# Eight weight buffers at eight different offsets modulo 512 bytes

## The chip, the core and the metric

The kernel runs on one core of a Trainium2 chip. The core has a matrix engine (TensorE, PE in the profile; its weight loads are PEld), a vector engine (VectorE, DVE), a scalar engine (ScalarE, ACT), GpSimd (POOL) and SyncE (SP), whose queue issues most of the DMAs here. They share SBUF, an on-chip memory of 128 partitions, in which a tile has the same byte range in every partition; TensorE writes its products to PSUM. The metric is the time of one execution on the device in microseconds (us).

## What is computed

A decoder trunk of two layers for 256 tokens and a model width of 2048, all in float32. Each layer is a mixer and then a gated feed-forward network (5632 wide) with a short convolution on its gate. The first mixer is a dilated attention of 8 heads beside a convolution module; the second is attention with forget gates (16 heads).

```python
for l in range(DEPTH):
    h = rmsnorm(x, norm_mix[l])
    if l % 2 == 0:
        x = x + even_mixer(h, positions, ev_w_in[e], ev_conv_w[e], ...)
    else:
        x = x + odd_mixer(h, od_w_in[o], od_b_f[o], od_w_out[o])
    h = rmsnorm(x, norm_ffn[l])
    x = x + conv_ffn(h, ffn_w_up[l], ffn_conv_w[l], ffn_w_down[l])
return rmsnorm(x, norm_final)

def conv_ffn(h, w_up, conv_w, w_down):
    g, u = jnp.split(h @ w_up, [D_FF], axis=-1)
    g = causal_dwconv(g, conv_w)
    return (jax.nn.silu(g) * u) @ w_down
```

Nearly all the work is in the products of `h` and of what is made of it with weight matrices, some 410 MB that are read once from HBM.

## The kernel before

A float32 product is made from rounded parts. Every weight and every activation is split into a high part, rounded to the type fp32r that TensorE is given, and a low part, the rest; a product is high x high + high x low + low x high.

**The weights' stream.** `stream` (L78) is a generator that every product draws its weights from. For four k-tiles (128 rows each) of a panel of 512 columns it issues one DMA of 1 MB from SyncE into a tile `raw` (three buffers, L85). Each half of it, two k-tiles or 1024 columns of a partition, is split: ScalarE's cast makes the high part `whi` (L93) and VectorE subtracts it from `raw` to make the low part `wlo` (L94). Of `whi` and `wlo` there are four buffers each, in turn, in the pool `wp`. A buffer has 1024 float32 values, 4096 bytes in each partition, and they lie one behind another, so all eight begin at the same offset modulo 512 bytes: 64. The three `raw` buffers begin at 64 as well.

**Who reads the parts.** `panel_b` (L108) has the weights as the stationary operand, 128 x 128 at a time, and the activations as the moving one. In its wide form (L102, issued in a written order by `in_order`) each block of weights gives a pair: the high part with a 512-wide moving operand, which holds the activations' high and low parts side by side, and the low part with the 256 columns of the high part alone. In its narrow form (L122 to L124) it issues three matmuls of 256 columns. `panel_a` and the last product (`mm_a`, L136 to L138) have it the other way round: the activations are stationary, and 512 columns of weights move. The blocks of a buffer are 512 bytes apart, so every block keeps its buffer's offset modulo 512.

**The activations' tiles.** `xs`, the split input of a mixer or a network, begins at 64 modulo 512. It feeds the products ag, q, k, v and fl of the mixers and g and u of the networks (the letters stand behind `acc_`, `whi_`, `wlo_` and `raw_` in the profile). The attention's output `y` feeds the output projections: at 288 oa and ob in the first layer, at 416 oc in the second. The network's hidden tiles `hp` feed the down projection: at 448 in the first layer (d, `panel_b`), at 0 in the second (d by `panel_a`, then e).

**The last product.** The second layer's second group of the down projection (e, in `down1`) draws the last four k-tiles of its four panels into rooms taken from other tiles and, by `from_weights`, from `whi` and `wlo`.

The order on TensorE is that of the products; ScalarE and VectorE split weights ahead of it, as far as the four buffers allow, and do the normalisations, the softmax and the convolutions between.

Of the kernel before, what the change touches and what calls it, by code (L numbers as in the profile page):

```python
# [10 lines left out]
F32R = mybir.dt.float32r  # L11
# [5 lines left out]
P = 128  # L17
# [12 lines left out]
KC = 2  # L30
# [11 lines left out]
def trunk(ctx, tc, a):  # L42
# [4 lines left out]
    wp = ctx.enter_context(tc.tile_pool(name="wp", bufs=4))  # L47
# [4 lines left out]
    def misc(name):  # L52
        return pms.tile([P, 512], F32, tag="misc", name=name)
# [16 lines left out]
    def fill_in(after):  # L70
        pace[1] += pace[0]
        with tc.issue_after(after.ins), tc.high_priority(offset=-BEHIND):
            while waiting and pace[1] >= 1:
                waiting.pop(0)()
                pace[1] -= 1
        pace[1] = min(pace[1], 1.0)

    def stream(src_of, nk, width, name, dk=4, room=None):  # L78

        half = KC * 512 // width  # L80
        for c in range(0, nk, dk * 512 // width):
            n = dk * 512 // width
            raw = wp.tile([P, 2 * KC * 512], F32, tag="raw", name=f"raw_{name}_{c}", bufs=3)
            rv = raw[:, :n * width].rearrange("p (k c) -> p k c", k=n)
            loads.append(nc.sync.dma_start(out=rv, in_=src_of(c, n)))  # L85
            for h in range(0, n, half):
                if room is None:
                    hi = wp.tile([P, half, width], F32R, tag="whi", name=f"whi_{name}_{c + h}")
                    lo = wp.tile([P, half, width], F32R, tag="wlo", name=f"wlo_{name}_{c + h}")
                else:  # L90
                    hi, lo = room(f"{name}_{c + h}")
                with tc.high_priority(offset=AHEAD):
                    S.copy(hi, rv[:, h:h + half, :])  # L93
                    last = V.tensor_tensor(out=lo, in0=rv[:, h:h + half, :], in1=hi.bitcast(F32), op=ALU.subtract)  # L94
                fill_in(last)
                yield list(range(c + h, c + h + half)), hi, lo
# [38 lines left out]
    def mm_a(o, hi, lo, xh, xl, first, last):  # L135
        PE.matmul(o, xh, hi, start=first, stop=False)  # L136
        PE.matmul(o, xh, lo, start=False, stop=False)  # L137
        PE.matmul(o, xl, hi, start=False, stop=last)  # L138

    def panel_a(src_of, x2, kts, name):  # L140

        acc = [pacc.tile([P, 512], F32, tag="acc", name=f"acc_{name}_{t}") for t in range(2)]
        for ks, hi, lo in stream(src_of, len(kts), 512, name):
            for t in range(2):
                ts = slice(t * P, (t + 1) * P)
                for j, k in enumerate(ks):
                    x = x2(kts[k])
                    mm_a(acc[t], hi[:, j, :], lo[:, j, :], x[:, 0, ts], x[:, 1, ts], k == 0, k == len(kts) - 1)
        return acc

    def cols(w, panel, k0=0):

        def part(c, n):
            kt = k0 // P + c
            return w[panel, kt // 4, :, kt % 4:kt % 4 + n, :]
        return part
# [125 lines left out]
    with ExitStack() as ph:  # L282
# [72 lines left out]
        with tc.high_priority(offset=400):  # L355
            for i in range(4):
                t, h = divmod(i, 2)
# [259 lines left out]
    def x_back():  # L617
        for kt in range(0, KT, 2):
            tx = misc(f"tb_{kt}")
            for t in range(2):  # L620
                for k in range(2):
                    PE.transpose(tx[:, t * T + k * P:t * T + (k + 1) * P], xT[:, kt + k, t * P:(t + 1) * P], ident)
            S.copy(o[:, :, kt * P:(kt + 2) * P], tx.rearrange("p (t c) -> p t c", t=2))
        S.dma_start(out=gb, in_=a["norm_final"].partition_broadcast(P))

    def add_o(acc, t, i):
        cs = slice(512 * i, 512 * (i + 1))
        V.tensor_tensor(out=o[:, t, cs], in0=acc, in1=o[:, t, cs], op=ALU.add)

    def down1(gi, w_dn, k0, kts, g2, fp):  # L630
        if gi == 0:
            x_back()
            for i in range(4):
                acc = panel_a(cols(w_dn, i, k0=k0), g2, kts, f"d1{gi}{i}")
                for t in range(2):
                    add_o(acc[t], t, i)
            return


        with tc.issue_after(copies[-1].ins):  # L640
            S.activation(dummy, ones[:, 0:1], AF.Sqrt)
        acc = [[None, None] for i in range(4)]
        for b, (i, t) in enumerate((i, t) for i in range(4) for t in range(2)):
            acc[i][t] = misc(f"acc_e{i}{t}") if b < 3 else pacc.tile([P, 512], F32, tag="acc", name=f"acc_e{i}{t}")
        n = len(kts)

        def rows(i, t, at, ks, hi, lo):
            for j, k in enumerate(ks):
                kt, ts = kts[at + k], slice(t * P, (t + 1) * P)
                mm_a(acc[i][t], hi[:, j, :], lo[:, j, :], g2(kt)[:, 0, ts], g2(kt)[:, 1, ts], at + k == 0, at + k == n - 1)  # L650

        def part(i, at, k, **kw):
            return stream(cols(w_dn, i, k0=k0 + at * P), k, 512, f"e{i}_{at}", dk=k, **kw)

        for at in range(0, n - 4, 4):
            for i in range(4):
                for got in part(i, at, 4):
                    for t in range(2):
                        rows(i, t, at, *got)


        def from_gate(nm):
            return [fp.tile([P, KC, 512], F32R, tag=tag, name=f"{w}_{nm}", bufs=2) for tag, w in (("gp", "whi"), ("cv", "wlo"))]

        def from_hidden(nm):
            both = fp.tile([P, 4, 2, T], F32R, tag="hp", name=f"wboth_{nm}", bufs=6).rearrange("p a b t -> p (a b t)")
            return [both[:, 1024 * h:1024 * (h + 1)].rearrange("p (k c) -> p k c", k=KC) for h in range(2)]

        def from_weights(nm):
            return [wp.tile([P, KC, 512], F32R, tag=w, name=f"{w}_{nm}") for w in ("whi", "wlo")]  # L670

        def from_raw(nm):
            both = wp.tile([P, 2 * KC * 512], F32, tag="raw", name=f"wboth_{nm}", bufs=3).bitcast(F32R)
            return [both[:, 1024 * h:1024 * (h + 1)].rearrange("p (k c) -> p k c", k=KC) for h in range(2)]

        rooms = [from_gate] * 2 + [from_hidden] + [from_weights] * 4 + [from_raw]
        at = n - 4
        last = [list(part(i, at, 4, room=lambda nm: rooms.pop(0)(nm))) for i in range(4)]
        for t in range(2):
            for i in range(4):  # L680
                for got in last[i]:
                    rows(i, t, at, *got)
                add_o(acc[i][t], t, i)
                cs = slice(512 * i, 512 * (i + 1))
                S.activation(junk[:, 512 * (i % 2):512 * (i % 2) + 512], o[:, t, cs], AF.Square, accum_out=fs[:, t, i:i + 1])
                if i < 3:
                    V.tensor_tensor(out=o[:, t, cs], in0=o[:, t, cs], in1=gb[:, cs], op=ALU.mult)
            V.reduce_sum(out=sf[:, t:t + 1], in_=fs[:, t, :], axis=AX.X)
            rf = rsqrt_cols(sf[:, t:t + 1], 1.0 / D, f"fin{t}", 1)
            for i in (1, 0, 3, 2):  # L690
                cs = slice(512 * i, 512 * (i + 1))
                if i == 3:
                    V.scalar_tensor_tensor(out=o[:, t, cs], in0=o[:, t, cs], scalar=rf, in1=gb[:, cs], op0=ALU.mult, op1=ALU.mult)
                elif i == 1:
                    V.tensor_scalar(out=o[:, t, cs], in0=o[:, t, cs], scalar1=rf, scalar2=None, op0=ALU.mult)
                else:
                    S.activation(o[:, t, cs], o[:, t, cs], AF.Copy, scale=rf)
                nc.sync.dma_start(out=a["out"][t * P:(t + 1) * P, cs], in_=o[:, t, cs])
# [63 lines left out]
```

## Time and profile before

| | |
|---|---|
| time, median of 3 runs | 2226.87 us (2223.21 to 2228.09) |
| profiled execution | 2227.58 us, of it span 2225.8 us |
| granted TensorE clock, mean | 0.997 |
| mean DMA rate | 186 GB/s |
| HBM read | 409.84 MB |

The span is the time from the first instruction of the program to the last one's end. A group of the profile is the set of instructions of one line, engine, operation and tiles; behind its count stand busy time, mean ns of one, and the idle time of the engine just ahead of them with what ended it. The end of a matmul in the profile is modelled, and successive matmuls overlap, so the pace of TensorE is read from starts: the length of a stretch divided by the matmuls that began in it. A stretch is written as start:end in us from the span's beginning. The count behind TensorE's busy time is of all matmuls that touch the stretch, so one that began before it can be among them.

### The profile page before, as it was taken

The page shows a single profiled execution, that of the slowest core. Times are in us where ns is not written, and L with a number is a line of the kernel's source. Part 1 is how long each engine was busy: PE and PEld are TensorE (multiplying, and loading weights), DVE is VectorE, ACT ScalarE, POOL GpSimd, SP SyncE. Part 2 cuts the span into 40 slices and gives each one's busy share as a digit, 9 for nine tenths or more (in the row PEclk, how much of TensorE's full clock was granted, in tenths as well). Part 3 has the DMA queues.
Part 4 walks back from the last instruction along what each step waited for, and adds up shares of the span by engine and source line. Part 5 has one row for each costly group of instructions (what it writes and reads, how often), then busy time and mean ns, then how long its engine had stood idle before and what let it go on. Part 6 is the DMA issues. An engine that isn't in the chain of part 4 may idle for free.

```text
span 2225.8 us, 31945 instructions
## 1 busy us (share of the span) xinstructions
PE 2206.7 (99%) x12778; PEld 1944.7 (87%) x12778; DVE 1490.9 (67%) x2284; ACT 1118.0 (50%) x1579; POOL 15.6 (1%) x50
## 2 busy tenths in 40 slices
PE   8999999999999999999999999999999999999998
PEld 8999988888888888888888888888888888888886
DVE  6999987766755576666665555666776644677745
ACT  6567665544443445444554454455454433444534
POOL 0000000000000000000000000000000000000000
PEclk9999999999999999999999999999999999999999
DMA  8554445555555555555545444455555555555553
GB/s 284 184 186 173 152 174 186 189 190 190 189 188 189 189 189 190 189 190 189 191 156 187 171 171 169 178 184 200 184 189 191 192 194 192 189 190 189 190 189 133
DMA packets 60230, 414.08 MB, mean 186 GB/s; under 512 B 7232, under 2 KB 7936, under 8 KB 11184
## 3 DMA queue, kind: packets, MB, share of 16 engines
q1 hardware_dynamic: 59328, 410.72, 51.8%
q8 instruction: 100, 1.64, 0.3%
q10 hardware_dynamic: 144, 1.05, 0.1%
q0 software_dynamic: 608, 0.26, 0.1%
q14 instruction: 50, 0.41, 0.1%
HBM read 409.84 MB, written 2.10 MB: 185 GB/s over the span
## 4 chain that ended last, share of the span: by engine, by line
PE 98%; DMA 1%; ACT 1%; DVE 0%; SPq 0%; issue 0%; ACTq 0%; DVEq 0%
PE acc_g L102 22%; PE acc_u L102 22%; PE acc_d L102 11%; PE acc_oc L102 4%; PE acc_q L102 4%; PE acc_k L102 4%; PE acc_ob L102 2%; PE acc_d L136 2%; PE acc_d L138 2%; PE acc_v L137 2%; PE acc_v L138 2%; PE acc_v L136 2%; PE acc_d L137 2%; PE acc_e L137 2%; PE acc_e L136 2%; PE acc_e L138 2%
## 5 line engine op out<-in xcount | busy, mean ns | idle before, releaser
L102 PE MATMUL acc_g<-xs,whi_g 128*128 128x512 f32 x1408 | 490.7, 392 | 0.0
L102 PE MATMUL acc_u<-xs,whi_u 128*128 128x512 f32 x1408 | 489.8, 392 | 0.0
L102 PE MATMUL acc_g<-xs,wlo_g 128*128 128x256 f32 x1408 | 394.1, 280 | 0.0
L102 PE MATMUL acc_u<-xs,wlo_u 128*128 128x256 f32 x1408 | 393.4, 279 | 0.0
L94 DVE TENSOR_TENSOR wlo_g<-raw_g,whi_g 128x1024 fp32r<-128x1024 f32 x176 | 215.3, 1223 | 165.5 <-ACT whi_g L93 165.2
L102 PEld LDWEIGHTS acc_g<-xs,whi_g 128*128 128x128 f32 x1408 | 263.6, 187 | 59.5 <-issue 0.5
L102 PEld LDWEIGHTS acc_u<-xs,whi_u 128*128 128x128 f32 x1408 | 263.5, 187 | 58.8
L93 ACT CAST whi_u<-raw_u 128x1024 fp32r<-128x1024 f32 x176 | 185.7, 1055 | 254.5 <-PE acc_u L102 142.1
L94 DVE TENSOR_TENSOR wlo_u<-raw_u,whi_u 128x1024 fp32r<-128x1024 f32 x176 | 215.4, 1224 | 124.4 <-ACT whi_u L93 124.4
L93 ACT CAST whi_g<-raw_g 128x1024 fp32r<-128x1024 f32 x176 | 185.3, 1053 | 213.8 <-PE acc_g L102 99.1
L94 DVE TENSOR_TENSOR wlo_d<-raw_d,whi_d 128x1024 fp32r<-128x1024 f32 x136 | 166.5, 1224 | 162.4 <-ACT whi_d L93 162.0
L102 PEld LDWEIGHTS acc_g<-xs,wlo_g 128*128 128x128 f32 x1408 | 265.8, 189 | 0.1
L102 PEld LDWEIGHTS acc_u<-xs,wlo_u 128*128 128x128 f32 x1408 | 265.7, 189 | 0.0
L93 ACT CAST whi_d<-raw_d 128x1024 fp32r<-128x1024 f32 x136 | 143.0, 1051 | 212.3 <-PE acc_d L102 126.7
L102 PE MATMUL acc_d<-hp,whi_d 128*128 128x512 f32 x704 | 247.9, 394 | 0.0
L102 PE MATMUL acc_d<-hp,wlo_d 128*128 128x256 f32 x704 | 199.1, 283 | 0.0
L102 PEld LDWEIGHTS acc_d<-hp,whi_d 128*128 128x128 f32 x704 | 132.2, 188 | 31.4 <-issue 1.1
L102 PEld LDWEIGHTS acc_d<-hp,wlo_d 128*128 128x128 f32 x704 | 132.4, 188 | 0.0
L102 PE MATMUL acc_q<-xs,whi_q 128*128 128x512 f32 x256 | 90.5, 395 | 0.0
L102 PE MATMUL acc_oc<-y,whi_oc 128*128 128x512 f32 x256 | 90.3, 395 | 0.0
L102 PE MATMUL acc_k<-xs,whi_k 128*128 128x512 f32 x256 | 88.9, 391 | 0.0
L94 DVE TENSOR_TENSOR wlo_v<-raw_v,whi_v 128x1024 fp32r<-128x1024 f32 x48 | 58.7, 1222 | 45.1 <-ACT whi_v L93 44.4
(317 smaller groups left out, 4200.1 us busy)
## 6 DMA issues: line engine op xcount, KB each, us to landing
raw_g<-in_ffn_w_up SPq DMA_DIRECT2D x88, 1024.0 KB, 4.7
raw_u<-in_ffn_w_up SPq DMA_DIRECT2D x88, 1024.0 KB, 4.8
raw_d<-in_ffn_w_down SPq DMA_DIRECT2D x68, 1024.0 KB, 4.7
raw_e<-in_ffn_w_down SPq DMA_DIRECT2D x20, 1024.0 KB, 4.8
raw_q<-in_od_w_in SPq DMA_DIRECT2D x16, 1024.0 KB, 4.8
raw_k<-in_od_w_in SPq DMA_DIRECT2D x16, 1024.0 KB, 4.8
raw_v<-in_od_w_in SPq DMA_DIRECT2D x16, 1024.0 KB, 4.8
raw_oc<-in_od_w_out SPq DMA_DIRECT2D x16, 1024.0 KB, 4.8
```

The lines of the kernel that those rows point to most:

```text
L93: S.copy(hi, rv[:, h:h + half, :])
L94: last = V.tensor_tensor(out=lo, in0=rv[:, h:h + half, :], in1=hi.bitcast(F32), op=ALU.subtract)
L102: i = PE.matmul(*args, **kw).ins
L136: PE.matmul(o, xh, hi, start=first, stop=False)
L137: PE.matmul(o, xh, lo, start=False, stop=False)
L138: PE.matmul(o, xl, hi, start=False, stop=last)
```

## The change

The tiles `whi` and `wlo` get 16 more float32 values each (64 bytes in each partition), which nothing reads or writes. A new function `split_pair` makes both tiles and gives views of their first 1024 values; `stream` and `from_weights` call it.

```diff
+    def split_pair(nm, half, width):
+
+        both = [wp.tile([P, KC * 512 + 16], F32R, tag=w, name=f"{w}_{nm}") for w in ("whi", "wlo")]
+        return [t[:, :KC * 512].rearrange("p (k c) -> p k c", k=half) for t in both]
+
     def stream(src_of, nk, width, name, dk=4, room=None):
...
                 if room is None:
-                    hi = wp.tile([P, half, width], F32R, tag="whi", name=f"whi_{name}_{c + h}")
-                    lo = wp.tile([P, half, width], F32R, tag="wlo", name=f"wlo_{name}_{c + h}")
+                    hi, lo = split_pair(f"{name}_{c + h}", half, width)
...
         def from_weights(nm):
-            return [wp.tile([P, KC, 512], F32R, tag=w, name=f"{w}_{nm}") for w in ("whi", "wlo")]
+            return split_pair(nm, KC, 512)
```

A buffer is now 4160 bytes, 8 x 512 + 64, so each begins 64 bytes further on modulo 512 than the one before it:

| buffers in the order in which they lie | before | after |
|---|---|---|
| `whi`, four | 64, 64, 64, 64 | 64, 128, 192, 256 |
| `wlo`, four | 64, 64, 64, 64 | 320, 384, 448, 0 |

The high and the low part of the same weights stand 256 apart modulo 512 in each of the four pairs. The tiles below the buffers (`xs`, `xT`, `raw`, constants) stay where they are; all that is allocated above them moves up by 512 bytes. The instructions of every engine and their order are the same in both programs.

## The prediction

> **What bounds the kernel now.** I read the page's head first, then its groups, then stretches of single products.
>
> ```profile
> span 2225.8 us, 31945 instructions
> PE 2206.7 (99%) x12778; PEld 1944.7 (87%) x12778; DVE 1490.9 (67%) x2284; ACT 1118.0 (50%) x1579; POOL 15.6 (1%) x50
> PEclk9999999999999999999999999999999999999999
> PE 98%; DMA 1%; ACT 1%; DVE 0%; SPq 0%; issue 0%; ACTq 0%; DVEq 0%
> ...
> L102 PE MATMUL acc_g<-xs,whi_g 128*128 128x512 f32 x1408 | 490.7, 392 | 0.0
> L102 PE MATMUL acc_u<-xs,whi_u 128*128 128x512 f32 x1408 | 489.8, 392 | 0.0
> ...
> L94 DVE TENSOR_TENSOR wlo_u<-raw_u,whi_u 128x1024 fp32r<-128x1024 f32 x176 | 215.4, 1224 | 124.4 <-ACT whi_u L93 124.4
> L93 ACT CAST whi_g<-raw_g 128x1024 fp32r<-128x1024 f32 x176 | 185.3, 1053 | 213.8 <-PE acc_g L102 99.1
> ```
>
> TensorE is busy 99% of the span at the full granted clock and is 98% of the chain that ended last; its large groups stand idle for 0.0 us. ScalarE's cast, which makes the high part of the weights, waits for TensorE: 213.8 us of idle over 176 casts is 1.2 us before each, and the largest releaser is a matmul that gives a buffer back. So the weights are ready early, and only the pace of the matmuls sets the time.
>
> That pace isn't in the durations, since matmuls overlap. It is in the starts. The next rows are stretches of one product each with nothing but matmuls in them; the columns are the stretch, its length, TensorE's busy time with the matmuls that touch it, the granted clock and the DMA share.
>
> ```profile
> 397.42:419.61 22.19, 22.19 (x128) 1.00 0.55 193
> 1907.16:1929.35 22.19, 22.19 (x128) 1.00 0.52 185
> 1118.16:1140.35 22.19, 22.19 (x128) 1.00 0.54 191
> 619.29:641.75 22.46, 22.46 (x129) 1.00 0.52 191
> 976.48:998.94 22.46, 22.46 (x129) 1.00 0.54 191
> 1460.49:1481.27 20.78, 20.78 (x120) 1.00 0.54 185
> 319.37:330.46 11.09, 11.09 (x64) 1.00 0.54 189
> 152.08:186.64 34.56, 34.56 (x288) 1.00 0.47 165
> 268.60:278.66 10.06, 10.06 (x86) 1.00 0.35 112
> 225.74:242.54 16.80, 16.80 (x75) 1.00 0.50 183
> 1753.12:1884.97 131.85, 131.85 (x576) 1.00 0.54 191
> ```
>
> Rows 1 to 3 are a gate panel (g), an up panel (u) and a key panel (k) of the second layer. Each has 64 pairs of a 512-wide matmul (high part) and a 256-wide one (low part): 22.19 / 64 = 346.7 ns a pair, three times the same. Rows 4 and 5 are panels of the first layer's down projection (d) with the same 64 pairs (the 129th matmul began before): 350.9 ns. Row 6 is the odd layer's output projection (oc): of the 120 matmuls that touch the stretch one began before it, so 119 steps from start to start take 20.78 us, 174.6 ns each, and 349.2 ns a pair. Row 7 is ob, the B half of the even layer's output projection: likewise 63 steps in 11.09 us, 352.1 ns a pair. Instructions, shapes and weights' buffers are alike in all seven; the moving operand differs. It is xs in g, u and k, which begins at 64 modulo 512 bytes, as all eight weights' buffers do. It is hp at 448 in d, y at 416 in oc, y at 288 in ob. **The pair is quickest where both operands begin at the same offset, and 2.5 to 5.4 ns slower in the three products where they don't.** ScalarE, VectorE and the DMAs aren't the cause: they are at work in all of these rows.
>
> The last four rows are other forms. Row 8, keys of the first layer (256-wide alone, xs at 64): 34.56 / 288 = 120.0 ns a matmul. Row 9, oa (256-wide, y at 288): 85 steps in 10.06 us, 118.4 ns; there the unequal offsets are the quicker. Row 10, values (weights move, xs is stationary at 64): 74 steps in 16.80 us, 227.0 ns. Row 11, the second half of the second layer's network, first group (weights move, hp is stationary at 0): 131.85 / 576 = 228.9 ns.
>
> The weight loads say that two streams meet. In the next rows, from the instructions that touch one accumulator, the numbers are shortest, median and longest ns.
>
> ```profile
> L102 PE MATMUL acc_k<-xs,whi_k x256: 391/391/391, 1118.2 to 1361.5; 128*128 128x512 f32 x128
> L102 PE MATMUL acc_d<-hp,whi_d x704: 387/396/479, 619.3 to 1088.8; 128*128 128x512 f32 x176
> L122 PEld LDWEIGHTS acc_q<-xs,whi_q x128: 192/192/192, 101.1 to 151.6; 128*128 128x128 f32 x128
> L122 PEld LDWEIGHTS acc_oa<-y,whi_oa x128: 187/188/192, 251.7 to 302.2; 128*128 128x128 f32 x128
> ```
>
> With equal offsets all 256 matmuls take 391 ns to the nanosecond, and a load in the narrow form always 192. With other offsets the same shapes wander from 387 upward, and the load from 187. I read this as the load of the next weights and the moving operand of the running matmul holding each other up in SBUF, locked into one pattern where the offsets agree.
>
> **The change part by part.** No instruction is added, removed or moved on any engine, and no wait changes. Each of the eight buffers grows by 64 bytes, so that they begin at 64, 128, 192, 256 (high parts) and 320, 384, 448, 0 (low parts). All that lies above them moves by exactly 512 bytes and keeps its offset; raw and xs don't move. The cost of the space is nothing.
>
> *Wide pairs on xs.* From the page 1408 + 1408, and 256 each of the second layer's q and k, and 16 of the forget gates: 3344 pairs, now at equal offsets. Afterwards seven loads in eight have another offset than xs. What a pair then costs more is in rows 4 to 7: 4.2 (d), 2.5 (oc) and 5.4 ns (ob), where the weights stand 128, 160 and 288 bytes past the moving operand, modulo 512. New here are 64, 192, 256, 320, 384 and 448 too, which no wide row shows. I take the mean, 4.0 ns: 3344 x 7/8 x 4.0 = +11.7 us. Bounds: nothing, if only the moving operand's own place counts, and twice the largest row, 10.8 ns, for offsets not seen: +31.6 us. Below nothing see the second rival.
>
> *Narrow matmuls on xs.* 8 panels (ag, q, k) of 192: 1536 x 7/8 x (118.4 - 120.0) = -2.2 us; at most 0.
>
> *Values.* 576 matmuls from 227.0 towards 228.9: 576 x 7/8 x 1.9 = +1.0 us.
>
> *Products that are unequal already.* 1088 wide pairs (d, oc, ob), the narrow oa and 1056 matmuls of the second layer's down projection change from one unequal offset to several. I take 0; rows 6 and 7 lie 1.5 ns either side of their middle, so 1.6 us either way for the pairs, and 2.0 us (1.9 ns x 1056) for the rest.
>
> *Writers.* The cast and the subtraction write the moved buffers. At 1053 and 1224 ns, with 1.2 us of idle ahead of a cast, some ns more or less stay under TensorE's work. The cover would be gone only if a cast and a subtraction grew by more than that 1.2 us together; then TensorE would wait at every buffer.
>
> Sum: 11.7 - 2.2 + 1.0 = **+10.5 us**. The profiled execution took 2227.58 us (2225.8 us of span and 1.8 us around it), 0.7 us above the median of the runs shown, 2226.87. That gives 2238.1 us.
>
> **The rivals.**
>
> *No change, 2227 us.* The difference between g and d then comes from where the moving operand lies, not from how it stands to the weights; xs doesn't move, so g, u, q and k keep 346.7 ns. Or the memory repeats at 64 bytes, and all eight offsets are one. Left is the values' +1.0 and at most -2.2: about 2227. For it: d and ob differ from g in the address of the moving operand alone, so the trace can't part the two readings for wide pairs. Against it: rows 10 and 11 have the weights moving at 64 in both, and only the stationary operand's offset differs (64 and 0), by 1.9 ns.
>
> The Trainium skill has a rule for this rival: "TensorE: Matmul & The Clock Gate", Part 2, step 1, says that TensorE reads SBUF through two independent ports, so that loading the next weights doesn't take read bandwidth from the running matmul. By it the sum would be 0 and the time 2227. The rows of acc_k and acc_d above, equal shapes at 391 and 396 ns, and loads of 192 and 188 ns speak for some contact between the streams, though not for its place.
>
> *Faster, 2210 us.* In the narrow form equal offsets are the slow case: both streams begin in step and meet in every load. If that is the general effect and the wide rows 4 to 7 are slow for their moving operand's own place, every matmul on changed weights gains the 1.6 ns of rows 8 and 9: 8864 in wide pairs, 1920 narrow and 1632 with moving weights are 12416 x 7/8 x 1.6 = -17.4 us. It decides from the point where a wide pair on xs falls below 346.7 ns. For it: the locked load of 192 ns against 188. Against it: three products out of three with wide pairs are slower than g.
>
> **How the numbers follow.** A measurement of this kernel can tell about 0.2%, 4.5 us, from no change. Forecast (slower by 5 to 31 us): 0.54. No change: 0.27, of which a little is the forecast at its smallest. Faster: 0.19, half of it below -13 us. The likeliest is the forecast, 2238 us; its own range is 2232 to 2258. For 8 in 10 the range reaches over no change to the upper half of the faster case, 2214, and to 2258, where the doubled excess lies.
>
> **What would show it.** A panel of g, u or second-layer k should take 22.19 + 64 x 7/8 x 4.0 ns = 22.41 us, its matmuls no longer 391 ns throughout but spread as in acc_d; the first layer's q and k should have loads under 192 ns and 118 to 120 ns a matmul; values 228 to 229 ns; d, oc and ob stay within 1.5 ns. If g's panels are 22.19 still, the place of the moving operand was the cause; if they are under 22.1, equal offsets were the worst choice. A change of waits, of the cast's idle time or of the DMA share would say that the reasoning looks at the wrong thing altogether.

## The result, and the profile after

| | before | after |
|---|---|---|
| time, median | 2227.48 us (2223.21 to 2231.07, 4 runs) | 2240.60 us (2238.59 to 2242.36, 4 runs) |
| profiled execution, its span | 2227.58, 2225.8 us | 2238.59, 2236.8 us |

The ratio is 1.006 (95% interval 1.0047 to 1.0074): the changed kernel is 0.6% slower. The order of instructions on every engine is the same.

First the page of the changed kernel: its head, the first line of the chain that ended last, and the groups that answer to those of before (busy time, mean ns of one, idle time ahead of them). All lines of the program lie four further down, so L102 is now L106.

```profile
span 2236.8 us, 31945 instructions
PE 2217.9 (99%) x12778; PEld 1941.6 (87%) x12778; DVE 1491.0 (67%) x2284; ACT 1116.1 (50%) x1579; POOL 15.6 (1%) x50
...
PE 98%; DMA 1%; ACT 1%; DVE 0%; SPq 0%; issue 0%; ACTq 0%; DVEq 0%
...
L106 PE MATMUL acc_g<-xs,whi_g 128*128 128x512 f32 x1408 | 496.9, 396 | 0.0
L106 PE MATMUL acc_u<-xs,whi_u 128*128 128x512 f32 x1408 | 496.7, 396 | 0.0
...
L98 DVE TENSOR_TENSOR wlo_u<-raw_u,whi_u 128x1024 fp32r<-128x1024 f32 x176 | 215.2, 1223 | 130.5 <-ACT whi_u L97 130.3
L97 ACT CAST whi_g<-raw_g 128x1024 fp32r<-128x1024 f32 x176 | 184.7, 1049 | 221.1 <-PE acc_g L106 103.1
```

TensorE is still the chain, with no idle time ahead of its matmuls; it is busy 11.2 us longer and the span grew by 11.0. The writers take what they took (1049 and 1223 ns, 1053 and 1224 before) and wait longer for TensorE (221.1 us of idle ahead of the cast of g, 213.8 before). So the time is where the prediction looked for it, in the pace of the matmuls.

Next the stretches of single products, matmuls alone, columns as before: g, the second layer's k, the first layer's d, oc and ob, the narrow k, the values, and the second layer's d.

```profile
434.71:457.23 22.52, 22.52 (x128) 1.00 0.51 188
1341.79:1364.31 22.52, 22.52 (x128) 1.00 0.54 186
684.30:717.73 33.43, 33.43 (x192) 1.00 0.54 189
1440.68:1462.69 22.01, 22.01 (x128) 1.00 0.54 192
311.49:322.31 10.82, 10.82 (x63) 1.00 0.54 194
146.39:179.92 33.53, 33.53 (x288) 1.00 0.49 170
218.99:236.08 17.09, 17.09 (x75) 1.00 0.51 181
1758.64:1891.69 133.05, 133.05 (x576) 1.00 0.54 189
```

A panel of g or k has 64 pairs: 351.9 ns a pair instead of 346.7. In d 190 steps from start to start take 33.43 us, 351.9 ns a pair (350.9 before); in oc 126 steps, 349.4 (350.0 before); in ob 62 steps, 349.0 (353.4 before). These two figures of before are from one 512-wide start to the next; the stretches in the prediction hold an odd number of steps, so their 349.2 and 352.1 count one short step too many. A narrow matmul takes 116.4 ns (120.0), one of the values 231 ns (74 steps; 227.0 before), one of the second layer's down projection 231.0 (228.9).

Within a panel the pace now changes with the buffer. A buffer serves eight pairs; these are the four buffers of the first half of the g panel above.

```profile
434.71:437.54 2.83, 2.83 (x16) 1.00 0.33 139
437.54:440.36 2.82, 2.82 (x18) 1.00 0.62 203
440.36:443.15 2.79, 2.79 (x18) 1.00 0.42 176
443.15:445.97 2.82, 2.82 (x18) 1.00 0.74 238
```

From starts with more digits that is 353.8, 352.1, 348.9 and 352.8 ns a pair, and the second half of the panel repeats it. In this order the high parts stand 0, 192, 128 and 64 bytes past `xs`. No buffer is at 346.7 any more, not even that whose high part still lies at 64 as `xs` does.

Lastly, product by product: the time from the first start of each panel to the last, summed over the panels, after less before. Between the panels nothing changed beyond 0.3 us in all.

| products | predicted, us | measured, us |
|---|---|---|
| wide pairs on xs (g, u, second-layer q and k, fl) | +11.7 | +15.2 |
| narrow on xs (ag, q, k; with the gaps between) | -2.2 | -7.1 |
| values | +1.0 | +2.0 |
| d, oc, ob, oa (oa ±0.0, d +0.5, oc -0.2, ob -1.8) | 0 | -1.5 |
| second layer's down projection (d and e) | 0 | +2.2 |
| sum | +10.5 | +10.8 |

The first matmul starts 0.2 us later, which makes the span's 11.0.

Two stretches of before, TensorE alone, belong to this table: one in ag, one at the start of ob.

```profile
35.77:39.20 3.43, 3.43 (x18) 0.50 0.53 160
305.05:309.20 4.15, 4.15 (x15) 0.59 0.16 32
```

The granted clock was 0.50 and 0.59 there, and 1.00 in the same places of the changed kernel. Narrow matmuls took 213 ns in the first stretch, and five pairs 640 ns in the second. That is about 1.4 us each that before's profiled execution lost by its clock and not by offsets. At an equal clock the narrow products gain about 5.7 us, the fourth row is near 0, and the change costs some 13.6 us, near the 13.1 us between the medians.

### The profile page after: what moved, and what is told of

It is laid out like the page before. It is cut to its first block, busy times and chain, and to the rows that moved or that the text cites. A ratio compares the mean times of both kernels' runs of the same rounds, so it can differ in the third digit from the quotient of the medians.

```text
span 2236.8 us, 31945 instructions
## 1 busy us (share of the span) xinstructions
PE 2217.9 (99%) x12778; PEld 1941.6 (87%) x12778; DVE 1491.0 (67%) x2284; ACT 1116.1 (50%) x1579; POOL 15.6 (1%) x50
## 4 chain that ended last, share of the span: by engine, by line
PE 98%; DMA 1%; ACT 1%; DVE 0%; SPq 0%; issue 0%; ACTq 0%; DVEq 0%
PE acc_g L106 22%; PE acc_u L106 22%; PE acc_d L106 11%; PE acc_q L106 4%; PE acc_k L106 4%; PE acc_oc L106 4%; PE acc_ob L106 2%; PE acc_v L140 2%; PE acc_v L142 2%; PE acc_d L141 2%; PE acc_d L142 2%; PE acc_v L141 2%; PE acc_d L140 2%; PE acc_e L141 2%; PE acc_e L142 2%; PE acc_e L140 2%
## 5 line engine op out<-in xcount | busy, mean ns | idle before, releaser
L106 PE MATMUL acc_g<-xs,whi_g 128*128 128x512 f32 x1408 | 496.9, 396 | 0.0
L106 PE MATMUL acc_u<-xs,whi_u 128*128 128x512 f32 x1408 | 496.7, 396 | 0.0
L106 PE MATMUL acc_g<-xs,wlo_g 128*128 128x256 f32 x1408 | 396.4, 282 | 0.0
L106 PE MATMUL acc_u<-xs,wlo_u 128*128 128x256 f32 x1408 | 395.9, 281 | 0.0
L106 PEld LDWEIGHTS acc_g<-xs,whi_g 128*128 128x128 f32 x1408 | 264.6, 188 | 63.4 <-issue 0.6
L106 PEld LDWEIGHTS acc_u<-xs,whi_u 128*128 128x128 f32 x1408 | 264.6, 188 | 63.2
L98 DVE TENSOR_TENSOR wlo_u<-raw_u,whi_u 128x1024 fp32r<-128x1024 f32 x176 | 215.2, 1223 | 130.5 <-ACT whi_u L97 130.3
L97 ACT CAST whi_g<-raw_g 128x1024 fp32r<-128x1024 f32 x176 | 184.7, 1049 | 221.1 <-PE acc_g L106 103.1
L98 DVE TENSOR_TENSOR wlo_d<-raw_d,whi_d 128x1024 fp32r<-128x1024 f32 x136 | 166.4, 1224 | 164.4 <-ACT whi_d L97 164.2
L106 PEld LDWEIGHTS acc_g<-xs,wlo_g 128*128 128x128 f32 x1408 | 265.0, 188 | 0.1
L106 PEld LDWEIGHTS acc_u<-xs,wlo_u 128*128 128x128 f32 x1408 | 265.0, 188 | 0.0
L97 ACT CAST whi_d<-raw_d 128x1024 fp32r<-128x1024 f32 x136 | 142.7, 1049 | 214.6 <-PE acc_d L106 127.3
L106 PE MATMUL acc_d<-hp,whi_d 128*128 128x512 f32 x704 | 248.4, 396 | 0.0
L106 PE MATMUL acc_d<-hp,wlo_d 128*128 128x256 f32 x704 | 197.9, 281 | 0.0
L106 PEld LDWEIGHTS acc_d<-hp,whi_d 128*128 128x128 f32 x704 | 132.3, 188 | 32.4 <-issue 1.1
L106 PEld LDWEIGHTS acc_d<-hp,wlo_d 128*128 128x128 f32 x704 | 132.5, 188 | 0.0
L106 PE MATMUL acc_q<-xs,whi_q 128*128 128x512 f32 x256 | 91.1, 396 | 0.0
L106 PE MATMUL acc_k<-xs,whi_k 128*128 128x512 f32 x256 | 90.3, 396 | 0.0
L106 PE MATMUL acc_oc<-y,whi_oc 128*128 128x512 f32 x256 | 90.1, 395 | 0.0
L98 DVE TENSOR_TENSOR wlo_v<-raw_v,whi_v 128x1024 fp32r<-128x1024 f32 x48 | 58.7, 1224 | 46.4 <-ACT whi_v L97 46.3
```

Of the source, the lines that this page charges most:

```text
L106: i = PE.matmul(*args, **kw).ins
```

## The experiments

The prediction says that a pair is quickest where weights and activations begin at the same offset. Its terms are off by some us each, and the buffer with the equal offset isn't quick. Below, a *distance* is the offset of a weights' buffer less that of the activations, modulo 512, and (a,b) stands for the distances of the high and the low part. Before, every product on `xs` was at (0,0).

**All eight buffers at 448.** Everything else keeps its offset, so `xs` is at distance 384 from the weights, and the first layer's hp (448) at 0.

```diff
+                    if len(loads) == 1 and h == 0:
+                        wp.tile([P, 96], F32, tag="ahead", name="ahead", bufs=1)
+                    hi = wp.tile([P, half, width], F32R, tag="whi", name=f"whi_{name}_{c + h}")
+                    lo = wp.tile([P, half, width], F32R, tag="wlo", name=f"wlo_{name}_{c + h}")
+                    if len(loads) == 1 and h == 0:
+                        wp.tile([P, 32], F32, tag="behind", name="behind", bufs=1)
```

> All eight weight buffers begin at 448 modulo 512 instead of 64, alike again; everything else keeps its offset. Pair theory (the distance of the stationary from the moving operand, modulo 512, sets the pace): the first layer's down projection d, whose moving operand is at 448, now has distance 0 and its clean panels fall from 22.46 to 22.19 us; the panels of g, u and the second layer's k, whose moving operand is at 64, rise from 22.19 to 22.35-22.6 us; the narrow matmuls of q and k fall from 120.0 ns to 116-119; time 2230 to 2240 us. Own-place theory (64 is a good place for weights, whatever they meet): g, u, k and d all rise alike, d above 22.46. Mixture theory (it costs that neighbouring loads lie at different offsets): nothing changes, g at 22.19, d at 22.46, 2227 us.

Measured: 2243.12 us, ratio 1.0063 (1.004 to 1.0086), 3 us above the expected 2230 to 2240. The rows are of this run: a panel of g, and two stretches of d.

```profile
439.06:461.54 22.48, 22.48 (x128) 1.00 0.53 189
655.66:684.78 29.12, 29.12 (x170) 1.00 0.53 187
981.33:1005.36 24.03, 24.03 (x139) 1.00 0.53 181
```

g takes 351.1 ns a pair, with one offset for all buffers: a pair can be as slow as in the changed kernel without any mixing of offsets. And xs, which hasn't moved, is slow with other weights' offsets, so it isn't the moving operand's own place either: **the distance counts**. (That it isn't the weights' own place is shown further down, where hp moves under weights that stay.) d at distance 0 takes 346.7 ns in the first stretch (84 pairs) but 353.3 in the second (68 pairs): the same distance has two steady paces. That was no part of any theory. It stands in the trace of before as well, in the second layer's g:

```profile
1532.76:1549.72 16.96, 16.96 (x98) 1.00 0.57 205
```

These 48 pairs at equal offsets take 353.3 ns each. The panel ahead of it and the first halves of the networks' first g panels are like it. Where it changes can be seen pair by pair; these are the times in ns from one 512-wide matmul's start to the next, in the middle of the first layer's first g panel of before:

```
360 350 350 360 350 350 360 350 350 360 796 352 347 346 347 347 346 347 347 346 347
```

A pattern of three pairs, 353.3 ns on average, runs until one pair is interrupted: in the 796 ns four small matmuls of the normalisation (`ss_f`) stand between its two. From then on every pair takes 346 or 347.

**A sweep of distances.** The four buffers of the high parts, and those of the low parts, become one block each with 512 bytes to spare, and every product has its own offset in it. The waits where the offset moves make the whole longer (2315.39 and 2316.85 us), so only the paces count.

```diff
+            blocks.extend(wp.tile([P, 4 * KC * 512 + 128], F32R, tag=w, name=w, bufs=1) for w in ("whi", "wlo"))
+        turn[0] = (turn[0] + 1) % 4
+        at = [o // 4 + turn[0] * KC * 512 for o in offsets(name)]
+        return [b[:, i:i + KC * 512].rearrange("p (k c) -> p k c", k=half) for b, i in zip(blocks, at)]
```

> Each product has its own offset of the weights (the four buffers of a kind slide together), so that one run gives the pace against the distance; the whole time says little. Pair theory: a wide pair of g and u takes 346.7 ns at distance 0 and 349 to 354 at others; d with its weights moved by 384 bytes, oc by 352 and ob by 224 have distance 0 and fall to 346.7 as well; the mean over the four combinations of the change (high part moved by 0, 64, 128, 192, low part by 256 more) is 351.9, what the changed kernel has. Own-place theory: d, oc and ob follow g's curve by the weights' offset, and have their best at 0. Mixture theory: every panel with one offset for high and low parts takes 346.7 ns for g and u, and only the panels with two are slower.

> As the first sweep, with other combinations; the 22 combinations of g and u are run in both layers, in another order, so each meets another predecessor. One pace for a distance: a combination takes the same in both layers. Lock theory: a good part of the combinations differ between the layers, by jumps between the values seen so far (340.0, 344.5, 346.7, 348.9, 350.0, 351.1, 353.3 ns), never by values between. For the narrow matmuls four panels have the weights moved by 64: 113.3 ns each by the first theory, some at 117.8 (which 320 gave) by the second. In the last product (weights move by 448 to distance 0 from the stationary tile) 226.7 ns against 228.9.

Both kernels differ in the offsets alone. Four stretches of the first one, of a wide product at (32,32), (128,128) and (448,0), and of a narrow one at (64,64):

```profile
392.03:411.47 19.44, 19.44 (x112) 1.00 0.53 182
459.43:478.73 19.30, 19.30 (x112) 1.00 0.55 183
1802.48:1821.18 18.70, 18.70 (x112) 1.00 0.55 191
38.14:56.95 18.81, 18.81 (x168) 1.00 0.65 241
```

The first three hold 110 steps, 55 pairs: 353.5, 350.9 and **340.0 ns**; the fourth 166 steps, 113.3 ns a matmul. Unequal offsets can be 6.7 ns quicker than the equal ones of before. Settled paces in ns, read in this way from both sweeps, to 0.3 ns ("or" where the same distance showed two; other unequal pairs were tried too, and gave values between the same ends):

| distances | wide pair on xs |
|---|---|
| (0,0), (256,256) | 346.7 or 353.3, 353.3 |
| (32,32), (288,288) | 353.2, 353.5 |
| (64,64), (320,320) | 353.2, 353.2 |
| (96,96), (352,352) | 346.8, 346.8 |
| (128,128), (384,384) | 351.1, 351.0 |
| (160,160), (416,416) | 350.0, 350.0 |
| (192,192), (448,448) | 353.3, 348.9 or 353.3 |
| (224,224), (480,480) | 346.9, 346.8 |
| (0,64), (0,128), (0,192) | 346.9, 350.0, 346.6 |
| (64,0), (128,0), (320,0) | 350.0, 352.0, 350.0 |
| (192,0), (448,0) | 340.2 or 350.0, 340.0 or 350.0 |

For the narrow form, distances 0, 64, 128 and 192 gave 119.9, 113.3, 118.6 and 117.8 ns, and 256, 320, 384 and 448 gave 120.0, 117.8, 118.6 and 117.8 (320 alone differs). Where the weights move, the same four gave 226.7 to 227.3, 229.0 to 229.4, 232.3 and 233.0 to 233.4 ns. Nearly every value comes back in product after product to 0.3 ns, or jumps to another of the same few: of the 21 combinations that the second sweep runs in both layers, six showed another pace in the second layer, the rest the same. Two expectations failed. Put at distance 0, d, oc and ob took 353.3 ns and not 346.7, the other pace of that distance. And the four combinations of the change, one by one, took 346.6, 353.3, 351.0 and 348.9 ns, on average 350.0 and not 351.9. The costs of the two parts don't add: (0,128) is 3.3 ns over 346.7 and (128,0) 5.3, but (128,128) is 4.4 over it. **The theory from here on: a lock.** TensorE's two reads, of the block to be loaded next and of the running matmul's columns, fall into a repeating pattern of stalls; the distances decide which patterns are stable, some allow two, and an interruption of the sequence, by a wait or by other matmuls, can change from one to the other. That stalls are behind the paces is argued from the paces alone; no run shows a stall itself.

**High parts at 0, low parts at 64.** If that is so, (448,0) with the four-buffer tiles of before must beat both kernels.

```diff
+                        wp.tile([P, 112], F32, tag="ahead", name="ahead", bufs=1)
+                    hi = wp.tile([P, half, width], F32R, tag="whi", name=f"whi_{name}_{c + h}")
+                    if len(loads) == 1 and h == 0:
+                        wp.tile([P, 16], F32, tag="between", name="between", bufs=1)
+                    lo = wp.tile([P, half, width], F32R, tag="wlo", name=f"wlo_{name}_{c + h}")
```

> All high parts begin at 0 and all low parts at 64 modulo 512; xs stays at 64. In the sweep one up panel with this combination took 340.2 ns a pair, the least of all, but another panel 128 bytes further had 350. Pair theory with one pace for a distance: every panel of g, u and the second layer's k takes 340.0 ns a pair, 21.76 us, which is 3344 x 6.7 = 22 us less; values lose some 2 us where the high parts move at distance 192, so 2205 to 2212 us. Lock theory (a distance allows more than one stable pace, and which one holds depends on what went before): some panels at 340.0 and others at 350.0 or above, a switch only behind a stall; 2205 to 2240 us. No-effect theory (the 340 was one panel's accident): 346.7 or 350 throughout, 2227 us or more.

Measured: 2211.18 us, ratio 0.9943 (0.9922 to 0.9964). A panel of g in the first layer and one of g in the second group of the second layer:

```profile
435.57:457.33 21.76, 21.76 (x128) 1.00 0.54 196
1955.36:1977.76 22.40, 22.40 (x128) 1.00 0.53 191
```

340.0 ns a pair in the first, and 350.0 in the second: the same distance again has two paces, and the ten panels behind the second layer's first down projection stay in the slow one to the end. The prediction's first sentence on the mechanism, that equal offsets are quickest, falls here.

**Only the high parts spread, only the low parts spread.** One block of four buffers gets the 64 bytes for each buffer, and a tile of 256 bytes behind keeps the rest in place. The diff is against the changed kernel and for the first of the two; the second has the two lines the other way round.

```diff
-        both = [wp.tile([P, KC * 512 + 16], F32R, tag=w, name=f"{w}_{nm}") for w in ("whi", "wlo")]
+                    hi = wp.tile([P, KC * 512 + 16], F32R, tag="whi", name=f"whi_{name}_{c + h}")[:, :KC * 512].rearrange("p (k c) -> p k c", k=half)
+                    lo = wp.tile([P, half, width], F32R, tag="wlo", name=f"wlo_{name}_{c + h}")
+                        wp.tile([P, 64], F32, tag="behind", name="behind", bufs=1)
```

> Only the four buffers of the high parts are spread (64, 128, 192, 256 modulo 512); the four of the low parts all begin at 320; what lies above keeps its offset. Distances to xs (high, low) are (0,256), (64,256), (128,256), (192,256). Theory of the lock (the pace belongs to the two distances together, out of a small set): a wide pair on xs takes the mean of four such paces; two were seen, 346.8 and 340.4, the other two are unseen and lie between 340.0 and 353.3, so 343.5 to 348.5 ns a pair, in groups of eight pairs of different pace, and 2217 to 2234 us. Rival, each spread costs by itself: the change's +5.2 ns a pair is the sum of what this kernel and the one with only the low parts spread add over 346.67; then one of the two must lie above 349 ns. Rival, the pace is the distance of the two loads that follow each other (high to low): not constant here, so spread as in the change, about 351.9 ns and 2240 us.

> Only the four buffers of the low parts are spread (64, 128, 192, 256 modulo 512); the four of the high parts all begin at 64, as xs does; what lies above keeps its offset. Distances to xs (high, low) are (0,0), (0,64), (0,128), (0,192). Theory of the lock: the sweep had 346.7 or 353.3, 346.95, 350.0 and 346.6 ns for these one by one, so 347.6 to 349.2 ns a pair in groups of eight pairs that differ, and 2228 to 2238 us. Rival, each spread costs by itself: this kernel and the one with only the high parts spread add up to +5.2 ns over 346.67. Rival, only the high part's distance counts: 346.67 throughout in wide pairs, 2223 to 2231 us.

Measured: 2232.65 us, ratio 1.0031 (1.002 to 1.0042), and 2234.82 us, ratio 1.0038 (1.0024 to 1.0051). A g panel takes 349.6 ns a pair in the first and 349.4 in the second. The expected 343.5 to 348.5 and 347.6 to 349.2 were both missed, on the slow side. Together the two excesses make 5.6 ns where the change has 5.2, so the rival of added costs, which fails in the sweep, isn't refuted by these two; for that they were a poor choice. The rival that only the high part's distance counts is: the second would have stayed at 346.67. What they show is in the buffers. In turn, a g panel of the first:

```profile
438.16:440.99 2.83, 2.83 (x16) 1.00 0.36 151
440.99:443.71 2.72, 2.72 (x18) 1.00 0.60 193
...
449.35:452.12 2.77, 2.77 (x18) 1.00 0.34 145
452.12:454.93 2.81, 2.81 (x19) 1.00 0.68 230
```

Rows 1 and 3 are the first and the second time the same buffer comes round, at (0,256): 354.1 and 346.6 ns a pair. Rows 2 and 4 are the next buffer, at (192,256): 340.6 and 350.5. With the buffers and the distances the same, both are at either of their two paces within one panel, and each of the four numbers lies within 1 ns of one that the sweep has for that distance modulo 256. I read this so: a buffer inherits the state in which the one before it left the engine, and the state decides which of its paces it takes. My expectations had taken the quick pace where there were two; that is the miss.

**The period is 256 bytes.** Two gaps of 256 bytes put the buffers at 64, 64, 320, 320 and 320, 320, 64, 64 modulo 512.

```diff
+            pair = [wp.tile([P, half, width], F32R, tag="whiA", name=f"whi_{nm}", bufs=2), None]
+                wp.tile([P, 64], F32, tag="gap0", name="gap0", bufs=1)
+                late.append(wp.tile([P, half, width], F32R, tag="whiB", name=f"whi_B0", bufs=2))
+            pair[1] = wp.tile([P, half, width], F32R, tag="wloA", name=f"wlo_{nm}", bufs=2)
+                wp.tile([P, 64], F32, tag="gap1", name="gap1", bufs=1)
...
+        return [hi, wp.tile([P, half, width], F32R, tag="wloB", name=f"wlo_{nm}", bufs=2)]
```

> The eight buffers stay 4096 bytes long and begin, by two gaps of 256 bytes, at 64, 64, 320, 320 (high parts) and 320, 320, 64, 64 (low parts) modulo 512, so that a buffer pair's distances to xs are (0,256) or (256,0) in turn; what lies above keeps its offset. If the pace repeats with 256 bytes (theory): every distance is 0 again, so narrow matmuls on xs take 120.0 ns, values 227 ns, the second layer's down projection 229 ns as in the kernel before, and a wide pair on xs sits at 346.7 or 353.3 ns and at nothing between in a settled stretch: 2225 to 2249 us. If it repeats with 512 only (rival): half of the reads stand at a distance as in the change, narrow 116 to 119 ns, wide groups with paces such as 349 to 352, values 229 to 233 ns.

Measured: 2226.57 us, ratio 0.9993 (0.9983 to 1.0003). A g panel of each group of the first layer, and a narrow one:

```profile
439.64:461.83 22.19, 22.19 (x128) 1.00 0.54 188
842.85:865.47 22.62, 22.62 (x128) 1.00 0.54 187
128.46:151.26 22.80, 22.80 (x193) 1.00 0.54 194
```

346.7 in the first group, 353.3 throughout the ten panels of the second, and 120.0 ns for a narrow matmul (190 steps); the second layer's values take 227.7 and its down projection 228.9 ns. These are the paces of before and nothing else. Offsets that differ by 256 count as equal here, for d, oc and oa too, which stand at other distances and keep their paces of before. The sweeps leave three places where 256 bytes did differ: narrow at 64 and 320, (0,128) at 350.0 against (0,384) at 346.7, and (0,192) at 346.6 against (0,448) at 350.0. Whether each of these is one distance with two paces isn't shown. Modulo 256 the change has only four offsets, and the high and low part of a buffer pair always share one.

**Nobody writes.** The changed kernel, but 20 of the first layer's 22 gate and up panels read the buffers that their group's first gate panel left. (The expectation says 18; by the edit the first up panel of each group reads them too.)

```diff
+            if name[:3] in ("g0_", "u0_") and name not in ("g0_0", "g0_6"):
+                for h in range(0, n, half):
+                    yield (list(range(c + h, c + h + half)),) + stay[(c + h) // half % 4]
+                continue
```

> The changed kernel with its eight offsets, but in the first layer all gate and up panels save the first of each group (18 of 22) load, cast and subtract nothing: they read the four buffer pairs that the group's first panel left, so these panels' sums are of other weights. In them ScalarE and VectorE write no weights and no weights come in by DMA; TensorE reads the same four pairs of offsets in the same rotation. Theory (TensorE's own two reads set the pace): 351.9 ns a pair, 22.52 us a panel, as in the changed kernel, with the same groups of eight pairs (353.8, 352.1, 349.0, 352.7). Rival, the writers of the moved buffers stand in the way of the reads: below 349 ns a pair there, 346.7 or less if they are all of it. No expectation on the whole time beyond some us for the waits where the loads begin again.

It ran once, in 2242.13 us. One row for such a panel and one for the changed kernel's, all engines: TensorE's busy time, its loads, VectorE, ScalarE, GpSimd, clock, DMA share, GB/s. The first is of this run, the second of the changed kernel.

```profile
438.13:460.65 22.52, 22.52 (x130) 19.65 (x129) 4.09 (x12) 2.92 (x8) 0.00 (x0) 1.00 0.00 1
```

```profile
434.71:457.23 22.52, 22.52 (x130) 19.65 (x129) 13.62 (x21) 11.01 (x16) 0.00 (x0) 1.00 0.51 188
```

VectorE falls from 13.62 to 4.09 us, ScalarE from 11.01 to 2.92, the DMAs from half of their time to nothing, and the panel takes 22.52 us to the last digit, its buffers 353.8, 352.1, 348.9 and 352.8 ns a pair as in the changed kernel. The rival of the writers is out: **the pace is between TensorE's own two reads.** The Trainium skill, "TensorE: Matmul & The Clock Gate", Part 2, step 1, has two independent read ports, by which loading the next weights takes no bandwidth from the running matmul. The runs differ: the same instructions take 21.76, 22.19, 22.52 or 22.62 us a panel, by where the stationary block lies and, at one and the same distance (22.19 and 22.62), by the pace that was entered.

**A version that uses it.** Blocks as in the sweep, high parts at (448) and low parts at (0), narrow products' parts at (64,64), and pads that put hp of the first layer and the second layer's y at 64 as `xs`.

```diff
+        narrow = name[:2] in ("ag", "q0", "k0") or name in ("q1", "k1")
+        at = [o // 4 + turn[0] * KC * 512 for o in ((128, 64) if narrow else (0, 0))]
...
+            if l == 0:
+                fp.tile([P, 16], F32, tag="pad", name="pad_ff0", bufs=1)
...
+        mx.tile([P, 24], F32, tag="pad", name="pad_mx1", bufs=1)
```

> Each kind of part is one block of four buffers, low parts at 64 and high parts at 0 modulo 512 (64 bytes below the activations); the narrow products' parts lie at 128 and 128; hp of the first layer, y of the second and y_mid are put at 64 modulo 512 by pads, so that d and oc stand as g does. Theory of the lock: 340.0 ns a pair in g, u, second-layer k and q, d and oc; narrow 113.3 ns a matmul instead of 117.7. From the kernel with high parts at 0 and low parts at 64 (2211.2 us): 704 pairs of d x 10 ns = 7.0 less, 256 of oc x 13 ns = 3.3 less, 1536 narrow ones x 4.4 ns = 6.8 less: 2194 us, if the pairs stay in the quick one of the two paces seen at this distance (340.0 and 350.0). If d or oc lock at 350.0 instead, up to 10 us more: 2204. Rival, products on hp and y are slow for their own place: 2204 to 2207 us. Rival, the block that stands for four buffers adds waits where the parts move (one step of 64 or 128 bytes): up to some us more at the three changes.

Measured: 2206.41 us (2201.25 to 2218.94, 6 runs), ratio 0.9924 (0.9896 to 0.9952): the fastest kernel of the study, 0.8% under the one before and, by the two ratios to it (0.9924 and 1.006), 1.4% under the changed one. It is 12 us over what was expected. In its profiled execution, of 2201.25 us, d and a narrow product read:

```profile
646.34:673.53 27.19, 27.19 (x162) 1.00 0.56 194
122.78:144.31 21.53, 21.53 (x192) 1.00 0.59 216
```

339.9 ns a pair in d (160 steps) where before had 350.9, and 113.3 ns in the narrow form (190 steps). In the kernel with high parts at 0, d had weights at the same offsets and stood at 350.0. Products on hp and on y take the pace of xs when they stand at its distance: the own place of neither operand matters. Part of the shortfall of this execution, 7 us, is seen: the fourth panel of d's second group and the second of oc are at 350.0 (80 and 64 pairs, 1.4 us), and the values and the second layer's down projection have gone to 234 ns, which the expectation had not priced against the kernel with high parts at 0 (234 and 232 there, so 2.5 ns x 1056 = 2.6 us). More than the rest is a wait: between the first layer's keys and values, where the parts move, 5.6 us pass without a matmul of a product (0.1 us in the kernel with high parts at 0), which fits the expectation's last rival; no run isolates it. Against it stands a gain that the sum didn't count: the wide panels of the second layer's second group took 350.0 there and take 340.0 here, 6.4 us. Its runs spread over 18 us; that they differ by the pace that long groups of panels settle in is likely, but only one of them has a trace.

**The same with a better place for the products whose weights move.** The second layer's hp begins at 0 modulo 256, and the first layer's values and oa take parts at 64, for the values (0,0). The diff is against the kernel above.

```diff
-            if l == 0:
-                fp.tile([P, 16], F32, tag="pad", name="pad_ff0", bufs=1)
+            fp.tile([P, 48 if l else 16], F32, tag="pad", name=f"pad_ff{l}", bufs=1)
+        still = name in ("v0", "v1") or name[:2] == "oa"
+        at = [o // 4 + turn[0] * KC * 512 for o in ((128, 64) if narrow else (64, 0) if still else (0, 0))]
```

> As the kernel with high parts at 0, low at 64, narrow at 128/128, but hp of the second layer begins at 0 modulo 256 instead of 64, so that where the weights move (second layer's down projection, 1056 matmuls) high parts stand at distance 0 and low parts at 64; and the first layer's values take parts at 64/64, distance 0. Theory (distance, period 256): d1 and e fall from 234.5 to 227 to 229 ns, 6.6 us less; the first layer's values from 233.6 to 227 ns, 1.3 us less, perhaps half of it given back where the parts move: 2194 us where the wide pairs stay at 340.0, and about 7 us under that kernel in each run. Rival, 234 ns comes from the weights' own place: no change, 2201 to 2211.

Measured: 2216.96 us (2210.47 to 2223.22, 9 runs), ratio 0.9947 (0.9931 to 0.9963): no gain. The values in the first layer settled at 226.7 to 227 ns as expected, but the second layer's down projection went only to 231.9: with the high part at distance 0 and the low part at 64 the mixture isn't the mean of 226.7 and 229. The kernel with high parts at 0 had the same distances there and the same 232.0, which should have told me. And in this execution the wide panels of the second layer's second group are at 350.0, where the kernel above had 340.0:

```profile
1954.39:1976.79 22.40, 22.40 (x128) 1.00 0.54 189
```

Ten panels of 64 pairs at 10 ns are 6.4 us, more than the 2.6 us (1056 x 2.5 ns) gained in the down projection. Which of the two states a group enters wasn't under my control in any run.

## Why the prediction was right, and where it was not

**What bounds the kernel** was right: TensorE's pace, with no wait involved. The writers stayed hidden, and the run in which nobody writes shows that they don't enter the pace at all.

**"The pair is quickest where both operands begin at the same offset"** was wrong. That the distance between the two operands counts, not the moving operand's place, is shown (the buffers at 448, the pads under hp and y). But distance 0 isn't special: 340.0 ns at (448,0), and two paces, 346.7 and 353.3, at 0 itself. The trace of before held both in the products on xs. I had read three stretches of 346.7 and none of the panels at 353.3. The direction was right because before stood, nearly always, in the quicker pace of its distance; that was luck and no part of the mechanism.

**Wide pairs on xs**, forecast at +11.7 us: the term was mis-sized. It had 7/8 of the pairs at 4.0 ns, the mean of d, oc and ob. Two of these rows were misread: oc stood at 350.0 and ob at 353.4, so the three are 4.2, 3.3 and 6.7 ns over 346.7, and their mean of 4.7 gives +13.8 us. Measured: 351.9 in every settled panel, 5.2 ns over 346.7, and +15.2 us; over all 3344 pairs 5.2 ns would be 17.4, but some panels of before stood at 353.3 already or were interrupted. The eighth that was to stay at 346.7 went to 353.8, probably since the state that the buffer before it leaves puts it in the slower pace; and distances 64 and 192, unseen before, are at 352.8 and 352.1. The bound, 31.6 us, held with room.

**Narrow matmuls on xs**, forecast at -2.2 us: mis-sized. The one row to price them by, oa, stands at one distance, and 64 is far quicker (113.3). The steady pace fell from 120.0 to 116.4, 5.5 us over 1536 matmuls; the other 1.6 us lie in the first four panels (ag), and about 1.4 of them are before's stretch at half the clock. The weight loads of q fell below 192 ns, to 188, as the prediction's last part asked.

**Values**, forecast at +1.0 us from the second layer's down projection: +2.0, a pace of 231 ns instead of 228.9. The reading of rows 10 and 11 was right (distances 0 and 64), the other two offsets cost more (232.3 and 233).

**"Products that are unequal already"**, 0 within 1.6 and 2.0 us: not shown to be 0. The second layer's down projection lost 2.2 us, just past its bound, for the same reason as the values. ob gained 1.8 us, of which about 1.4 are the second stretch at the lower clock; its pace of 349.0 is 4.4 ns under that of before, three times what "within 1.5 ns" allowed. d and oc, 1.0 and 0.6 ns off, kept to it.

The time came out near the forecast, 2238.59 us for the profiled execution against 2238.1, by luck: these errors cancel, +3.5, -4.9, +1.0, -1.5 and +2.2 make +0.3. Before's clock makes the measured sum about 2.8 us too small; at an equal clock the forecast of 10.5 us stands against about 13.6.

**The rivals.** No change fell: the pace doesn't repeat with 64 bytes (a narrow matmul takes 120.0 ns at 0 and 113.3 at 64), and with 256 it does in the kernel that tests it. The faster rival fell for this change. Its reason, that equal offsets are a slow case, holds in the narrow form (120.0, with 256 and 96 the slowest of its distances), and unequal offsets do make the wide form faster, at a distance that the change doesn't use.

What stays open: how the reads stall each other, so that a distance could be priced without a sweep, and what decides which of two paces is entered. In the panels where I followed a change pair by pair, in four kernels, it stood at an interruption in the middle of a product (350 to 340 at a pair of 800 ns, which holds four matmuls of the normalisation; 340 to 350 at two late pairs of 500 and 423 ns in a row; two of 499 and 423 ns left another panel at 340), but no run isolated that, and a product can also begin in the slow state without one.

## What to carry to other kernels

A kernel that TensorE bounds and that changes weights with every matmul has a free parameter: where the weights' tiles begin relative to the moving operand. Here it was worth 0.6% of the time one way and 0.8% the other. Read the pace from starts, panel by panel, over the whole trace and not in three stretches: a panel at another steady pace with the same instructions says that there are several states. Read the granted clock of every stretch before two executions are compared product by product. Choose the distance by a sweep inside one kernel, give all buffers of a product the same one, and expect that some distances hold two paces; spreading buffers over several offsets takes a mixture and doesn't avoid the bad ones.

## What the runs showed that I had not expected

Equal instructions on equal data sizes run at a handful of paces: 340.0, 344.4, 346.7, 348.9, 350.0, 351.1 and 353.3 ns a wide pair (4% from end to end; a few combinations stood between, such as 349.3 and 352.0), 113.3 to 120.0 ns a narrow matmul (6%), 226.7 to 236.7 ns with moving weights (4%). They go by the distance of the two operands in SBUF, modulo 256 as far as it was tested, and by the state that was entered. Behind 353.3 at distance 0 stands a pattern of three pairs, 350, 350 and 360 ns. One distance can hold two paces, 6.7 or 10 ns apart, each for ten panels on end. Where all buffers of a product have one distance, in the panels followed pair by pair, the pace changed only where the sequence was interrupted, or from one product to the next.
